# The score products of differential attention: four products of a block in another order

## The chip, the cores and the metric

The kernel runs on one core of a Trainium2 chip. The metric is the time of one execution on the device, in microseconds (us). TensorE is PE in the profile (its weight loads are PEld), VectorE is DVE, ScalarE is ACT, GpSimd is POOL, and SyncE, which issues the transfers, is SP.

## The reference

The kernel computes two layers of a bidirectional trunk over 256 latent tokens, with 256 context tokens in front, at a width of 1024. Each layer has a token mixer of three parts (an mLSTM, an HGRN2 and differential attention) and then a channel mixer: a dense SwiGLU in layer 0, and two of eight SwiGLU experts for each token in layer 1. The change touches the scores of the differential attention only. It has 4 heads; each head has two maps with 64 channels each, and its output is the difference of two softmaxes times the values:

```
s = einsum('ibhqd,ibhkd->ibhqk', q, k) * 64 ** -0.5     # i: the two maps, d: 64 channels
p = softmax(s, axis=-1)
out = einsum('bhqk,bhkv->bhqv', p[0] - lam * p[1], v)
```

In layer 0 the latent tokens attend to all 512 tokens and the context tokens to the 256 context tokens. In layer 1 only the latent's output is needed.

## The kernel before

Everything is worked on in tiles of 128 partitions. All large products are made in float32r, with each fp32 operand split into an upper and a lower part; an exact product is then the sum of three, upper by upper and the two mixed ones. Results go to eight PSUM banks of 128 x 512 (`bank`).

Differential attention goes through tiles of 128 queries (`tt`): four in layer 0 (0 and 1 are context with 256 keys, 2 and 3 are latent with 512), two in layer 1 (both with 512). For each tile it goes through four heads. So there are 16 score blocks in layer 0 and 8 in layer 1.

The operands of a score block lie so that a head needs four products instead of six. The keys of map `i` (`dk`) hold the upper part on one half of the partitions and the lower part on the other half; for map 0 the upper part is on partitions 0 to 63, for map 1 on 64 to 127 (the slices in `both`). The upper part of the queries (`qh`) is on both halves. So one product over all 128 partitions gives upper query by upper key plus upper query by lower key. A second product, over the 64 partitions that hold the upper part of the keys, adds lower query (`ql`) by upper key. Each map has a bank of its own (`pe[0]`, `pe[1]`, called `psc` in the profile).

From there a block goes on like this: VectorE takes the maximum of each row of each map (`mx`, line 1240), ScalarE makes the exponentials and their sums (`E`, `das`), and VectorE combines both maps into one matrix of weights (line 1249 and the two operations after it). `values` transposes these weights on TensorE (line 1259) and copies them (`pT`), and `weighted` multiplies them with the values (`po`) and scales the result (`oo`).

The text of the loop keeps these steps apart: after the scores of a block come two steps of other work that waits for TensorE (`tick(T_DA)`: pieces of the modulation, and the first half of the output projection, `py`), then `onward`, which does `weighted` for an older block and `values` for a block two places back. During the first query tile each block is followed by transposes of the mixer's other outputs (`mix_t`, line 1147). The framework arranges instructions by a planner with costs of its own, except in stretches that are marked as strict; the attention is not one of these. Semaphores and buffers come from the framework too.

Before the attention, the projections (`pr`, `pp`) fill TensorE. After it the rest of the output projection (`py`) follows, then the channel mixer. Weights come through buffers (`raw`) loaded by SyncE's queue, and are split by ScalarE (`whi`) and VectorE (`wlo`). The mLSTM earlier in each layer multiplies keys and queries of two heads over 64 partitions each, one head on each half, each into its own bank (`pS`); it also makes rows of stabilizers by products over 64 partitions (`pM`).

Of the kernel before, what the change touches and what calls it, by code (L numbers as in the profile page):

```python
# [12 lines left out]
F32 = mybir.dt.float32  # L13
# [8 lines left out]
P = 128  # L22
# [10 lines left out]
# column offsets of the fp32 constant table  # L33
# [4 lines left out]
C_TRI = 768                       # [t', t] = 1 where t' < t  # L38
C_IOTA = C_TRI + 128              # row 0..127 on every partition, then 128..255
C_LOW = C_IOTA + 256              # [e, j] = 1 where j < e, 64 columns  # L40
C_SEL = C_LOW + 64                # [32 g + e, e] = 1, 8 columns
C_END = C_SEL + 8
# columns of the sum matrices, per direction: 7 levels, the two outer ones; then ones
# [6 lines left out]
# GpSimd starts no DMAs: its ring of descriptors is as small as it can be  # L50
RING = 1024

# columns of the per-feature table
# [6 lines left out]
# columns of the per-row table  # L60
# [4 lines left out]
# steps of waiting work at each place where a chain leaves gaps  # L65
# [3 lines left out]
def constants():  # L69
# [14 lines left out]
    k = np.zeros((P, 11 * 128), np.float32)           # 7 level masks, the diagonal; two causal masks, the diagonal  # L84
# [16 lines left out]
    m[:, S_OUT:S_OUT + 128] = u > t                       # forward, before the boundary  # L101
    m[:, S_OUT + 128:S_OUT + 256] = u <= t                # forward, after it
    m[:, S_DIR + S_OUT:S_DIR + S_OUT + 128] = u >= t      # backward, queries
    m[:, S_DIR + S_OUT + 128:S_DIR + S_OUT + 256] = u < t  # backward, keys
# [5 lines left out]
def kernel(ctx: ExitStack, tc: tile.TileContext, t: dict, out: bass.AP):  # L110
    nc = tc.nc
    # where a chain of small steps decides, each engine keeps to the order of this text
# [61 lines left out]
    def load_row(gd):  # L174
        """A vector by column, in a place for weights."""
        g = wp.tile([P, 2, D], F32, tag="raw", bufs=4, name="rowg")
        row_in(g, *gd, nc.sync)
        return g
# [9 lines left out]
    def whl(src, put_off=None):  # L188
        """Both parts of weights; the second one by an engine that is named later, if put_off takes it."""
        h, l = hl_tile()  # L190
        ACT(h, src, AF.Copy)
        low = lambda op=TT: op(l, src, h.bitcast(F32), op=ALU.subtract)
        put_off.append(low) if put_off is not None else low()
        return h, l
# [7 lines left out]
    def rstd_of(pool, ss, n, scale, tag, bufs=1):  # L202
        """1 / sqrt(ss * scale + EPS), with a step of Newton's method."""
# [32 lines left out]
    def mod_piece(l, g, n):  # L236
        """A quarter of the rows of 2048 columns of the modulation, four column groups side by side."""
# [26 lines left out]
    def first_mods(c):  # L264
        """Shift and scale of two feature tiles of the first input, four blocks of rows side by side."""
# [23 lines left out]
    work = []  # L289

    def tick(n):
        """Goes on with n steps of the work that waits; the loads of the next piece are sent off early."""
        while n > 0 and work:
            for w in work[:2]:
                if not w[1]:
                    w[1] = True
                    next(w[0])
            try:
                next(work[0][0])
                n -= 1  # L300
            except StopIteration:
                work.pop(0)
# [11 lines left out]
    def mod_affine(l, which):  # L314
        # 0: scale of the mixer's input, 1: gate of its output, 2, 3: the same of the channel mixer
# [9 lines left out]
    def row_out(src, streams):  # L325
        """A vector by feature, for some streams, on its way to gate_in."""
# [8 lines left out]
    def row_in(dst, gd, streams, q=nc.sync):  # L335
        """The vector by column, on every partition."""
# [9 lines left out]
    def scaled(pool, x, bufs=4):  # L346
        """x over its root mean square, for some tiles of tokens."""
# [14 lines left out]
    def pre_steps(pool, xh, l, which, tiles, ks=range(KT)):  # L362
        """Shifts and scales, by feature, of the scaled tiles of tokens."""
# [25 lines left out]
    def post_steps(pool, tiles, cuts=1):  # L389
        """dst = x + gate * norm(ys side by side), for tiles of tokens (ys, x, gate, dst)."""  # L390
# [32 lines left out]
    class Start:  # L423
        """Four feature tiles of the next part: the context's tokens first, as soon as they are there."""
# [9 lines left out]
        def parts(self, sub=TT):  # L434
            """Both parts of the next tile."""
# [14 lines left out]
        def half(self, n, between=None, plan=0, some=range(KT), at=(), lag=0):  # L450
            """The products of half of the tokens; between them, steps of the other half's input."""
# [9 lines left out]
            for j, (w, pp) in enumerate(zip(self.w, self.banks)):  # L461
                late = []
                for k in some:
                    # a bank's first product clears what is written for all of its columns
# [19 lines left out]
    def tail(product, post, pool, X, nxt, fill, plan, start):  # L484
        """The last products of a part, tile by tile of tokens, each with its residual, and the next part's input."""
# [20 lines left out]
    def mixer(l, X, banks=None):  # L506
        """X: the residual stream by token tile (0, 1: context; 2, 3: latent). Its tile holds the mixer's
        output meanwhile."""
# [31 lines left out]
        if l == 0:  # L540
            with tc.tile_pool(name=f"pn{l}", bufs=1) as pn:
# [20 lines left out]
                def turned(xh, first, ks):  # L562
                    """Feature tiles of two tiles of tokens, two of them in a bank; the two that lie together are not used in turn."""
# [19 lines left out]
                def both_pairs(ks):  # L583
                    """The same of all tiles of tokens; a bank for each feature tile."""
# [49 lines left out]
        # -- projections; what the tensor engine does with their results waits until the next one is under way  # L634
# [6 lines left out]
        def fm(ci, n, toks, use, ws=None):  # L641
            """n feature tiles of weights, stationary; use(j, psum) takes [feature, token]."""
# [14 lines left out]
        def tm(ci, tiles, use):  # L657
            """512 columns of weights, moving; use(i, psum) takes [token, column]."""
# [17 lines left out]
        # ============ HGRN2: gates  # L676
# [5 lines left out]
        lbc = hx.tile([P, 2, 4], F32, name="lbc")     # per head pair: ln lb, ln(1-lb), 1-lb, -ln lb  # L682
# [23 lines left out]
        def use_hgf(d):  # L706
            def use(j, pp):
# [5 lines left out]
                STT(s, pp, 0.0, e, op0=ALU.min, op1=ALU.subtract)          # ln sigmoid(f)  # L713
                TT(e, s, pp, op=ALU.subtract)                              # ln sigmoid(-f)
# [6 lines left out]
                STT(s, s, lbc[:, j, 0:1], e, op0=ALU.max, op1=ALU.add)     # ln f  # L721
# [38 lines left out]
        # ============ HGRN2: the recurrence, by halves  # L760
        def sums_of(dst, i, d, c, cols, extra=()):
            """dst [channel, 128]: sums of ln f over tokens of tile i that `cols` picks."""
# [8 lines left out]
        def squares(v, name):  # L771
            """Sums of squares by token and head."""
# [11 lines left out]
        def hgrn():  # L784
            opart = X[:, :, 256:512]
            # boundaries between tiles: context to latent, and between the two tiles of each
# [31 lines left out]
            # the heads of a pair run side by side in the array, each into its own bank  # L818
            half = [slice(0, 64), slice(64, 128)]
            for p0 in range(qt[0], 4, 2):  # L820
# [3 lines left out]
                def weigh(pa, blocks):  # L824
                    """Adds the values of the token tiles that pa's blocks (at, source, query tile) weigh."""
# [32 lines left out]
            # inside a tile: each level's product holds keys at one half of each block, queries at the other;  # L858
            # queries of a pair of heads lie side by side, with zeros where the other head's channels are
# [77 lines left out]
        # ============ mLSTM  # L937
# [29 lines left out]
        # ============ what the rest of the mixer needs from its input  # L967
        dq = hx.tile([P, 4, 512], F32, tag="w8", bufs=3, name="dq")
        # both parts of the keys of each head and map; the lower one at the other half of the partitions
# [18 lines left out]
        def rotated(dst, x, pp):  # L988
            """The rotation of the latent's tokens, of x that pp holds too."""
# [52 lines left out]
        scans(g2, ones_r, g1, ALU.mult, ALU.add)                          # F  # L1042
        TT(g0[R, :], g0[R, :], g2[R, :], op=ALU.subtract)                 # b = i - F
        tick(T_SCAN)
        scans(g1, g0, g0, ALU.max, ALU.max)                               # M
        TT(g2[R, :], g2[R, :], g1[R, :], op=ALU.add)
        tick(T_SCAN)
        ACT(g2[R, :], g2[R, :], AF.Exp, scale=-1.0)                       # exp(-m)
        gh = hg.tile([64, 512], F32R, tag="at", bufs=4, name="gh")
        gl = hg.tile([64, 512], F32R, tag="at", bufs=4, name="gl")  # L1050
        ACT(gh, g1[R, :], AF.Copy, scale=-1.0)                            # -M, in two parts
# [12 lines left out]
        for h in range(4):  # L1064
            if h % 2 == 0:
                # k q of both heads, side by side
# [11 lines left out]
            for d in range(2):  # L1078
# [3 lines left out]
                # -M along rows; the second with the causal mask of each diagonal block  # L1082
# [56 lines left out]
        # ============ differential attention  # L1139
        raw_o = [load(t["w_out"][l, 0, g]) for g in range(2)]  # L1140

        def mix_t(k, i0, i1):
            """Feature tile k of the mixer's output, gated, in two parts, for tokens i0..i1."""
# [61 lines left out]
        def out_first(i):  # L1205
            """Half of the output projection of a tile of tokens."""
# [12 lines left out]
        def queries(tt):  # L1219
            """The upper part of the queries at both halves of the partitions, and the lower part."""  # L1220
# [9 lines left out]
        def scores(tt, h):  # L1230
            sn = 512 if tt >= 2 else 256
            pe = [bank("psc") for _ in range(2)]
            qh, ql = qs[tt]
            for i, a, _ in both:
# [704 lines left out]
```

## Time and profile before

| what | value |
|---|---|
| runs | 2222.86 us median of 3 (2218.38 to 2222.91) |
| profiled execution | span 2226.4 us |
| PE busy | 2138.0 us (96%) |
| PEld busy | 1690.9 us (76%) |
| DVE busy | 1566.9 us (70%) |
| ACT busy | 1249.7 us (56%) |
| transfers | 496.81 MB, mean 223 GB/s |

The profiled execution is one run of its own; its span goes from the first to the last instruction. A busy share is the time in which at least one instruction of the engine was under way. Products on PE are pipelined, so the next one can start before the record of the one before ends; the spacing of two starts says more than the length of one record. PEclk is the granted clock of TensorE, where 1.00 is 2.4 GHz and 0.50 is 1.2 GHz.

### The profile page before, as it was taken

The numbers are of one execution on the slowest core, as the hardware profiler recorded it, in microseconds if no ns is written. First come the engines' busy times: TensorE is split into PE (matmuls) and PEld (weight loads), VectorE is DVE, ScalarE is ACT, GpSimd is POOL, SyncE is SP. The second block draws the span as 40 slices with busy tenths as digits, with TensorE's granted clock in tenths as the row PEclk, the third lists the DMA queues.
The fourth block names the chain that finished last, engine by engine and source line by source line (L and its number), as shares of the span: only waits on it lengthen the run. The fifth ranks groups of instructions, "written<-read, shape, count | busy, mean of one in ns | idle before, by whom it ended". The sixth has DMA issues, their size and how long they took to land.

```text
span 2226.4 us, 27694 instructions
## 1 busy us (share of the span) xinstructions
PE 2138.0 (96%) x10532; PEld 1690.9 (76%) x10532; DVE 1566.9 (70%) x2145; ACT 1249.7 (56%) x1832; POOL 86.8 (4%) x82
## 2 busy tenths in 40 slices
PE   7998998999999999999987999999999999999997
PEld 4877666787788788877866888877777777777775
DVE  4758657672222345766678999788888888888887
ACT  3632435562222335634556787767777677676765
POOL 1000003000000001000112000000000000000000
PEclk9999998799999999999988999999999999999999
DMA  8430444046321331435427999899998999989992
GB/s 302 152 103 30 133 152 151 1 189 237 122 76 38 132 114 42 164 114 189 61 97 311 366 375 346 305 349 350 355 354 322 349 351 350 357 321 355 355 348 105
DMA packets 81356, 496.81 MB, mean 223 GB/s; under 512 B 17728, under 2 KB 18752, under 8 KB 23104
## 3 DMA queue, kind: packets, MB, share of 16 engines
q1 hardware_dynamic: 81216, 494.97, 61.1%
q8 instruction: 84, 1.38, 0.2%
q14 instruction: 56, 0.46, 0.1%
HBM read 492.81 MB, written 2.13 MB: 222 GB/s over the span
## 4 chain that ended last, share of the span: by engine, by line
PE 37%; DVE 7%; ACT 2%; DMA 2%; issue 2%; DVEq 0%; ACTq 0%
PE pg L117 22%; PE py L117 13%; DVE wlo L117 5%; ACT whi L117 1%; DMA raw<-w_eu 1%; PE ph L1710 1%; DMA raw<-w_ed 1%; PE pcb L117 0%; PE px L117 0%; DVE X L117 0%; PE psc L117 0%; PE po L117 0%; DVE qh L1227 0%; DMA X<-w_eu 0%; PE pt L1259 0%
## 5 line engine op out<-in xcount | busy, mean ns | idle before, releaser
L117 DVE TENSOR_TENSOR wlo<-raw,whi 128x1024 fp32r<-128x1024 f32 x815 | 958.9, 1222 | 189.7 <-ACT whi L117 179.6
L117 ACT ACTIVATE whi<-raw 128x1024 fp32r<-128x1024 f32 (+1 forms) x820 | 815.4, 1055 | 272.7 <-PE pgu L117 148.9
L117 PE MATMUL pg<-wlo,TH 128*128 128x512 f32 x896 | 363.4, 406 | 5.7 <-DVE wlo L117 2.0
L117 PE MATMUL pg<-whi,TH 128*128 128x512 f32 x896 | 355.6, 397 | 0.8 <-DVE cf L117 0.8
L117 PE MATMUL pg<-whi,TL 128*128 128x512 f32 x896 | 351.9, 393 | 0.0
L117 PE MATMUL py<-whi,hhl 128*128 128x512 f32 x896 | 289.2, 394 | 0.0
L117 PEld LDWEIGHTS pg<-wlo,TH 128*128 128x128 f32 x896 | 168.3, 188 | 63.5 <-DVE wlo L117 30.2
L117 PEld LDWEIGHTS pg<-whi,TH 128*128 128x128 f32 x896 | 168.3, 188 | 40.4 <-DVE cf L117 1.2
L117 PEld LDWEIGHTS py<-whi,hhl 128*128 128x128 f32 x896 | 168.2, 188 | 38.6
L117 PEld LDWEIGHTS pg<-whi,TL 128*128 128x128 f32 x896 | 168.5, 188 | 35.1
L117 PE MATMUL py<-wlo,hhl 128*128 128x512 f32 x448 | 176.5, 394 | 1.0 <-DVE wlo L117 0.8
L117 ACT ACTIVATE hhl<-ph 128x512 fp32r<-128x512 f32 x56 | 33.3, 595 | 168.7 <-PE ph L1710 168.7
L117 PE MATMUL pgu<-TH,whi 128*128 128x512 f32 x320 | 127.2, 397 | 0.0
L117 PE MATMUL pgu<-TL,whi 128*128 128x512 f32 x320 | 126.6, 396 | 0.0
L117 PE MATMUL pgu<-TH,wlo 128*128 128x512 f32 x320 | 126.5, 395 | 0.0
L117 PE MATMUL pp<-TH,whi 128*128 128x512 f32 (+1 forms) x304 | 116.7, 384 | 0.0
L117 PE MATMUL pp<-TL,whi 128*128 128x512 f32 (+1 forms) x304 | 111.0, 365 | 0.0
L117 PE MATMUL pp<-TH,wlo 128*128 128x512 f32 (+1 forms) x304 | 110.7, 364 | 0.0
L117 PEld LDWEIGHTS py<-wlo,hhl 128*128 128x128 f32 x448 | 84.0, 188 | 21.8 <-DVE wlo L117 2.8
L117 PE MATMUL pm<-raw,sc 128*32 128x512 f32 x384 | 60.5, 650 | 15.6 <-DVE ry L117 9.3
L117 PEld LDWEIGHTS pgu<-TH,whi 128*128 128x128 f32 x320 | 60.1, 188 | 19.2 <-ACT whi L117 3.4
L117 DVE TENSOR_TENSOR hhl<-ph,hhl 128x512 fp32r<-128x512 f32 x56 | 38.6, 689 | 50.9 <-ACT hhl L117 50.8
(342 smaller groups left out, 3229.0 us busy)
## 6 DMA issues: line engine op xcount, KB each, us to landing
raw<-w_eg SPq DMA_DIRECT2D x112, 1024.0 KB, 6.7
raw<-w_eu SPq DMA_DIRECT2D x111, 1024.0 KB, 6.9
raw<-w_ed SPq DMA_DIRECT2D x111, 1024.0 KB, 6.9
raw<-w_mod SPq DMA_DIRECT2D x40, 1024.0 KB, 5.0
raw<-w_fm SPq DMA_DIRECT2D x22, 1024.0 KB, 5.0
raw<-w_fg SPq DMA_DIRECT2D x11, 1024.0 KB, 4.8
raw<-w_fu SPq DMA_DIRECT2D x11, 1024.0 KB, 6.3
raw<-w_fd SPq DMA_DIRECT2D x11, 1024.0 KB, 4.8
```

The source lines that it names most:

```text
L117: ins = op(*args, **kw)
L1710: nc.tensor.transpose(ph[:, j, :], sg[:, j * P:(j + 1) * P], ident)
```

## The change

The four products of a score block are issued in another order. Before, each map had its product over 128 partitions and then its product over 64. Now both products over 128 partitions come first, and then both over 64, the first on partitions 0 to 63 and the second on 64 to 127. Operands, banks, sizes and the accumulation flags of each product are the same. Apart from this the diff only drops comments.

```
     pe = [bank("psc") for _ in range(2)]
     qh, ql = qs[tt]
+    k = [dk[h // 2][:, h % 2, i, 0:sn] for i in range(2)]
+    for i in range(2):
+        MM(pe[i][:, 0:sn], qh[:, i, h, :], k[i], start=True, stop=False)
     for i, a, _ in both:
-        k = dk[h // 2][:, h % 2, i, 0:sn]
-        MM(pe[i][:, 0:sn], qh[:, i, h, :], k, start=True, stop=False)
-        MM(pe[i][:, 0:sn], ql[a, h, :], k[a], start=False, stop=True)
+        MM(pe[i][:, 0:sn], ql[a, h, :], k[i][a], start=False, stop=True)
     mx = hx.tile([P, 2], F32, tag="da_m", bufs=3, name="mx")
```

## Rows read from the trace of the kernel before

**Rows 1.** Page, part 2: busy tenths and granted clock in 40 equal slices

```profile
PE   7998998999999999999987999999999999999997
...
PEclk9999998799999999999988999999999999999999
```

**Rows 2.** Stretch, length, busy us of PE, PEld, DVE, ACT, POOL, clock, DMA, GB/s

```profile
376.94:415.40 38.46, 38.16 (x114) 24.89 (x111) 27.09 (x69) 19.57 (x62) 8.30 (x7) 0.50 0.27 107
384.00:392.00 8.00, 8.00 (x27) 4.68 (x20) 7.69 (x17) 3.45 (x10) 3.79 (x3) 0.50 0.40 140
415.40:440.00 24.60, 24.60 (x132) 18.26 (x131) 17.98 (x49) 15.54 (x43) 0.00 (x0) 1.00 0.01 2
1127.90:1135.60 7.70, 7.70 (x24) 5.30 (x24) 3.71 (x12) 3.43 (x10) 0.73 (x1) 0.50 0.03 13
1135.60:1146.00 10.40, 10.40 (x53) 6.83 (x53) 8.05 (x20) 8.16 (x23) 0.73 (x1) 1.00 0.00 1
```

**Rows 3.** PE's waits, 360 to 460 us, then from 1110 us: us, times, longest

```profile
PE pm L117 <- DMA raw<-w_mod: 5.8, 1, 5.8
PE pt L1259 <- DVE dar L1249: 0.3, 1, 0.3
...
PE pt L1259 <- DVE E L117: 3.1, 1, 3.1
...
PE po L117 <- ACT pT L117: 1.4, 2, 0.7
```

**Rows 4.** Tile psc: its products over 128 partitions; who waited for the tile

```profile
L117 PE MATMUL psc<-dk,qh x48: 279/502/794, 363.8 to 1144.9; 128*128 128x512 f32 x32, 128*128 128x256 f32 x16
...
  DVE mx L1240: 20.2, 23
```

**Rows 5.** Timeline of PE, two blocks of layer 0: start, us, what

```profile
393.54 0.58 PE L117 MATMUL psc<-dk,ql 64*128 64x256 f32 x1
394.05 0.58 PE L117 MATMUL psc<-dk,qh 128*128 128x256 f32 x1
...
405.11 0.79 PE L117 MATMUL psc<-dk,ql 64*128 64x512 f32 x1
405.83 0.79 PE L117 MATMUL psc<-dk,qh 128*128 128x512 f32 x1
```

**Rows 6.** Timeline of PE, a block of layer 1

```profile
1138.38 0.50 PE L117 MATMUL psc<-dk,ql 64*128 64x512 f32 x1
1138.81 0.50 PE L117 MATMUL psc<-dk,qh 128*128 128x512 f32 x1
```

**Rows 7.** Timeline of PE and its weight loads in the mLSTM of layer 0

```profile
293.22 0.40 PE L117 MATMUL pp<-TH,wlo 128*128 128x512 f32 x1
293.54 0.18 PEld L117 LDWEIGHTS pM<-gh,ident_r 64*128 64x128 f32 x1 [0.37 <-ACT whi L117]
293.55 0.50 PE L117 MATMUL pM<-gh,ident_r 64*128 64x512 f32 x1
293.65 0.18 PEld L117 LDWEIGHTS pM<-gl,ident_r 64*128 64x128 f32 x1
293.88 0.39 PE L117 MATMUL pM<-gl,ident_r 64*128 64x512 f32 x1
...
294.11 0.39 PE L117 MATMUL pM<-gh,ident_r 64*128 64x512 f32 x1
```

**Rows 8.** Timeline of PE, products of the output projection at 0.50

```profile
412.79 0.63 PE L117 MATMUL py<-wlo,TH 128*128 128x512 f32 x1
413.21 0.63 PE L117 MATMUL py<-whi,TL 128*128 128x512 f32 x1
```

**Rows 9.** Timeline of weight loads, pairs of mLSTM products over 64 partitions (512 columns, fp32)

```profile
228.73 0.26 PEld L117 LDWEIGHTS pS<-X 64*128 64x128 f32 x2 [0.17 <-DVE bT L1059]
...
229.16 0.26 PEld L117 LDWEIGHTS pS<-X 64*128 64x128 f32 x2 [0.17 <-issue]
```

**Rows 10.** Chain of work that ended last: start, us, what (four fp32 products, 128 columns)

```profile
1140.82 0.44 PE pt L1259 x4
```

## The prediction

> **What bounds the kernel now.** I began with the page's slices of busy time [rows 1]. PE is at nine tenths in most slices, and the granted clock falls below 9 in only four of the 40 (55.7 us each). Three of these hold the changed line: slices 7 and 8 (334 to 445 us, layer 0) and slice 21 (1113 to 1169 us, layer 1). Next come the stretches [rows 2]. From 376.9 to 415.4 us PE is busy for 38.16 of 38.46 us at a granted clock of 0.50 (1.2 GHz); from 415.4 to 440 us all of 24.60 us at 1.00 (2.4 GHz). VectorE has 27.09 us of work in the first of these and does not set the pace. Then the waits [rows 3]: around layer 0's attention PE waits once 5.8 us for a weight transfer, before 376.9 us, and after that 0.3 us in all. Layer 1 is another matter: PE waits 3.1 us for VectorE right before its fourth score block, and later twice for ScalarE (1.4 us together). From the other side [rows 4], VectorE's row maxima waited 23 times and 20.2 us for the score products. So from 376.9 us in layer 0, and from 1127.9 us in layer 1, the order of products on PE sets the pace. Behind it PE stays busy slice after slice, and transfers use 0.01 of their engines from 415.4 to 440 us, so time won there should reach the end of the program.
>
> **What the change touches.** A score block is four products: high part of map 0 over 128 partitions (H0), low part of map 0 over 64 (L0), then H1 and L1. There are 24 blocks: there are 48 H products, 16 of them with 256 columns and 32 with 512 [rows 4], so 8 blocks with 256 columns and 16 with 512. The order becomes H0, H1, L0, L1. Nothing is added: no instruction, DMA or queue entry, and no new wait of PE, since each product goes to the bank that it went to before.
>
> **Price of a change between 128 and 64 rows.** At full clock L0 to H1 is 0.43 us (1138.38 to 1138.81) [rows 6]. Products of one shape follow each other in 0.23 us (293.88 to 294.11) [rows 7]. Each change therefore costs 0.20 us. Rows 7 show where it lies: the last product before a change takes 0.33 (293.22 to 293.55), 0.10 over, and the first one after it 0.33 (293.55 to 293.88), because its weights begin to load only at 293.54. At half clock the spacing is 0.51 us with 256 columns (393.54 to 394.05) and 0.72 with 512 (405.11 to 405.83) [rows 5], against 0.42 for one shape with 512 columns (412.79 to 413.21) [rows 8] and half of that, 0.21, with 256. A change costs 0.30 us there at either width.
>
> A block now has four changes (H0-L0, L0-H1, H1-L1, L1 to the next 128-row product). The new one has two, H1-L0 and L1 to the next. So two go: 0.40 us at full clock, 0.60 at half.
>
> H1 must not expose its weight load after H0, or half a change comes back. Rows 7 show the second weight load at 293.65 running while the first product, on the same 64 rows, is still under way. The Trainium skill ("TensorE: Matmul & The Clock Gate", Part 3: Packing small matmuls) says that a weight load overlaps a running matmul only where the row group differs; by that rule H1 would show its load, about 0.10 us a block, and the sum below would be some 2.5 us smaller (half a change, 0.10 in 8 blocks and 0.15 in 11). The trace disagrees with that rule, and I leave the term out.
>
> **The two low products side by side.** L0 uses partitions 0 to 63 and L1 64 to 127, each in its own bank. The program already has such pairs: for k q of two mLSTM heads, two weight loads come every 0.43 us (228.73, 229.16) with 512 columns in plain fp32 [rows 9], while plain fp32 products of 128 columns take 0.11 us each (four in 0.44) [rows 10], so 0.44 for 512 columns. Two per 0.43 means that the pair runs together. The bounds for the low pair are nothing saved (one after the other) and a whole product (0.23 at full clock; 0.42 and 0.21 at half). I take a start of the second one a weight load later, 0.11 us (293.54 to 293.65) [rows 7], twice that at half clock: saved are 0.12 (512, full), 0.20 (512, half) and nothing (256, half). The Trainium skill (the same page, the same section) has products in distinct row groups start about 4 ns apart; an estimate by it would save the whole product, the upper bound, about 3 us more over all blocks.
>
> **Sum.** The blocks are counted in PE's timeline by clock and width; rows 5 and 6 show one of each kind. Layer 0: its first two blocks, before 376.9 us, win nothing, since PE then waits for the transfer. Six blocks of 256 columns at half clock: 6 x 0.60 = 3.6. Three of 512 at half: 3 x 0.80 = 2.4. Five of 512 at full: 5 x 0.52 = 2.6. Together 8.6 us (7.4 to 11.1 by the bounds). Layer 1: the first three blocks win nothing (VectorE is late after them); of the other five, two begin at half clock (0.80 and about 0.70) and three run at full (1.56): 3.1 us (2.5 to 3.9). All: 11.7 us (9.9 to 15.0).
>
> **What is late next.** VectorE is busy 7.69 of 8.00 us between 384 and 392 [rows 2], so two of the half-clock blocks cannot shrink: minus 1.2 us. In the whole stretch, 38.46 less 6.0 leaves 32.5 us over 27.1 us of VectorE work, so it holds there on average. In layer 1 VectorE has 8.05 and ScalarE 8.16 of 10.40 us, and PE's two waits for ScalarE stand right behind the blocks: I give back 1.1 of 3.1. The first map's maximum starts a little later, since L0 is now third (it ends 0.23 + 0.33 + 0.33 = 0.89 us after the start of a full-clock block, against two spacings, 0.86), and the second map's earlier by about 0.5. Left over: 9.4 us.
>
> **The clock.** It stays at 0.50 from 376.9 to 415.4 us although PE counts as busy throughout, and comes back while PE runs out-projection products (two of them are rows 8), which have no changes. In layer 1 it came back at 1135.6, after 7.7 us [rows 2]. A stream with fewer changes can only look denser. What an earlier return is worth has VectorE as its limit: 32.5 - 27.1 = 5.4 us in layer 0, up to 2 in layer 1; at the other end it is nothing, or a loss if the return slips (last rival). I take 1.6 us, nearer to no change.
>
> Total 11.0 us. The profiled span, 2226.4, is 3.5 us over the median of the timed runs, 2222.86 (2218.38 to 2222.91), so there is nothing around it to add. I take the difference from the median: 2222.9 - 11.0 = 2211.9 us.
>
> **Rivals.**
> *The time turns into waits (0.17).* PE's wins are handed back because VectorE and ScalarE are next in line. For it: the 0.3 us wait for VectorE [rows 3], the full VectorE at 384 to 392, and the two ScalarE waits in layer 1. Against it: VectorE's 20.2 us of waiting for PE. Then only the full-clock blocks of layer 0 and a little of the rest stay, 2.6 + 1 = 3.6 us: 2219.3.
> *The clock returns early (0.15).* Fewer changes lift it inside the blocks: 9.4 + 5.4 + 2 = 16.8 us, so 2206.
> *The order is not kept (0.04).* Outside of its strict parts a planner arranges the program, and it might issue the four products otherwise, or move other work. PE's order in the trace is that of the text, which speaks against it. Nothing changes: 2222.9.
> *Slower: the clock returns later (0.05).* Of the 24.6 us of full-clock PE work up to 440 us [rows 2], each one that runs at 0.50 instead costs about one more. With 14.5 of them caught (most of the five blocks and what stands between them) the loss is 14.5 against the gain of 9.4: 2228. It decides as soon as over 9.4 us are caught. Against it: the run of out-projection products that goes before the return keeps its place in PE's order.
> The forecast itself has 0.59.
>
> **From this the numbers.** A change under 0.2% (4.4 us) cannot be told from none. Faster: 0.59 of the forecast and 0.15 of the early clock, and a fifth of the waits rival (0.03): 0.77. Slower: most of the late clock, and a little for a planner that moves other work: 0.06. The rest, 0.17, is no change. The range runs from 2203 (the upper bounds of the pair with the early clock) to 2220 (the waits rival).
>
> **What would show it.** Right: in a full-clock block H0 to H1 is 0.23 to 0.33 us, the two L start within about 0.1 us of each other, and the block from H0 to the next product takes 1.1 to 1.2 us rather than the four spacings of 0.42 to 0.43; at half clock with 256 columns about 1.4 rather than 2.0. Layer 0's last score product comes some 7 us earlier against its start at 376.9, and the experts' first products some 10 us earlier. The pair is wrong if L0 to L1 is 0.23 or more at full clock. The forecast is wrong if new PE waits for VectorE or ScalarE appear between the blocks, or if the granted clock stands at 0.50 for longer in layer 0, or if the win in attention is lost in a later wait for a transfer.

## The result, and the profile after

The kernel with the new order took 2214.55 us (median of 7 runs, 2211.65 to 2220.39), the kernel before 2223.7 us (7 runs, 2218.38 to 2231.2). The ratio is 0.995, with a 95% interval from 0.9936 to 0.9964: 9.15 us less by the medians, where 11.0 were forecast. The profiled executions lie 12.4 us apart, spans of 2226.4 and 2214.0 us. The one before was among the longer ones of its kernel, so the steps below, which are read from the two traces, add up to 12.4 and not to 9.15. One of the 12 executions of "before, wait filled" further down ran at a mean clock of 0.56 for 3481 us and is left out of that kernel's numbers.

Timeline of PE in the kernel after: start, us, what. First a full-clock block with 512 columns, then a half-clock block with 256, then one with 512; the line behind each is the product that follows the block.

```profile
408.60 0.71 PE L117 MATMUL psc<-dk,qh 128*128 128x512 f32 x2
409.24 0.51 PE L117 MATMUL psc<-dk,ql 64*128 64x512 f32 x2
409.68 0.71 PE L117 MATMUL po<-dv,pT 128*128 128x128 f32 x4
...
390.76 0.78 PE L117 MATMUL psc<-dk,qh 128*128 128x256 f32 x2
391.47 0.58 PE L117 MATMUL psc<-dk,ql 64*128 64x256 f32 x2
391.98 0.58 PE L117 MATMUL po<-dv,pT 128*128 128x128 f32 x1
...
400.88 1.20 PE L117 MATMUL psc<-dk,qh 128*128 128x512 f32 x2
402.01 0.79 PE L117 MATMUL psc<-dk,ql 64*128 64x512 f32 x2
402.74 0.53 PE L117 MATMUL po<-dv,pT 128*128 128x128 f32 x2
```

From the first H to the product behind the block it is now 1.08 us at full clock, 1.22 with 256 columns at half clock, and 1.86 with 512 columns at half clock. The same distances in the kernel before are 1.69, 2.02 and 2.88 us, which are four of the spacings of [rows 5, 6]. The two low products are one entry of two that takes 0.44 us at full clock until the next product starts, as long as one product between two changes (0.43 by [rows 6]). They run together: in the trace's records the second starts 3 to 4 ns behind the first in all 24 blocks, not 0.11 us.

PE's waits in the same stretches as [rows 3], 360 to 460 us, then 1105 to 1134 us (us in total, times, longest):

```profile
PE pm L117 <- DMA raw<-w_mod: 6.8, 1, 6.8
PE po L117 <- ACT pT L117: 2.2, 2, 1.2
PE pt L1261 <- DVE E L117: 1.4, 2, 0.9
PE pt L1261 <- DVE dar L1251: 0.7, 1, 0.7
...
PE pt L1261 <- DVE E L117: 3.5, 2, 3.1
PE po L117 <- ACT pT L117: 0.3, 1, 0.3
```

Layer 0 had 0.3 us of such waits behind the transfer and has 4.3 now (2.2 + 1.4 + 0.7). On the other side the row maxima wait less for the scores; this is the row of tile psc that answers to the last one of [rows 4]:

```profile
  DVE mx L1242: 6.6, 7
```

Stretches of layer 0 from the third score block to the end of the sixteenth, and of layer 1 from the fourth to the end of the eighth, with the columns of [rows 2]. First the kernel before:

```profile
376.94:434.43 57.49, 57.19 (x209) 38.14 (x205) 40.40 (x102) 31.62 (x94) 8.30 (x7) 0.67 0.18 72
1128.63:1145.74 17.11, 17.11 (x72) 11.14 (x71) 10.77 (x30) 11.26 (x29) 1.46 (x2) 0.80 0.01 2
```

Then the kernel after, with four pieces of layer 0 that show the clock:

```profile
377.74:422.62 44.88, 40.61 (x209) 29.50 (x205) 39.35 (x102) 30.23 (x90) 8.16 (x7) 0.80 0.23 91
1119.69:1132.82 13.13, 12.71 (x72) 8.93 (x70) 10.16 (x29) 10.61 (x28) 1.45 (x2) 0.87 0.01 2
...
372.00:384.00 12.00, 8.12 (x38) 4.58 (x38) 8.94 (x18) 5.62 (x17) 5.02 (x4) 0.57 0.98 402
384.00:388.00 4.00, 1.84 (x12) 1.18 (x10) 3.94 (x11) 2.71 (x9) 1.47 (x2) 1.00 0.91 334
388.00:404.00 16.00, 13.89 (x54) 9.89 (x54) 14.54 (x42) 9.75 (x33) 3.92 (x4) 0.57 0.01 4
404.00:440.00 36.00, 36.00 (x213) 29.02 (x213) 24.69 (x69) 24.49 (x66) 0.00 (x0) 1.00 0.00 1
```

The same 209 PE instructions take 44.88 us instead of 57.49, so layer 0 gives 12.61. Their order differs beyond the change in one product of the output projection only, which the planner put behind an earlier block. It splits in four. The lengths of its 14 blocks, read as above, add up to 29.23 us before and 16.76 after, 12.47 less. Of these, 10.9 are the blocks' own: six of 256 columns and three of 512 at half clock and five at full, as before (6 x 0.80 + 3 x 1.02 + 5 x 0.61). The other 1.6 are three blocks that now run at full clock (2 x (1.22 - 0.82) + 1.86 - 1.08). PE's remaining work in the stretch fell from 27.96 (57.19 - 29.23) to 23.85 us (40.61 - 16.76), 4.1 us less with nothing changed in it but the clock: it was at 0.50 up to 415.4 us in [rows 2], and is at 1.00 from 384 to 388 and from 404 us here. Waits took 4.0 us back. So 10.9 + 1.6 + 4.1 - 4.0 = 12.6.

How much of this hangs on the one execution of the kernel before can be seen in a kernel from the experiments below, with the new order in layer 1 alone. Up to layer 1's scores its PE instructions are those of the kernel before, in the same order. Its stretch from the third to the sixteenth block:

```profile
376.93:430.83 53.90, 52.66 (x209) 34.93 (x205) 40.33 (x102) 31.19 (x94) 8.27 (x7) 0.74 0.19 76
```

The old order took 57.49 and 53.90 us here, at a granted clock of 0.67 and 0.74. The new order took 44.88, 44.2 (the second profile) and 44.8 (new order in layer 0 alone). So layer 0 gives 9 to 13 us, by the execution that is taken for before.

From there to the end, in the first two traces: layer 0's third block started 0.8 us later, so the next stage starts 11.8 us earlier (479.46 to 467.64). Layer 1's first block starts only 8.9 us earlier (1115.05 to 1106.11). Layer 1's blocks bring it to 12.5 us at the experts' first products (1194.3 to 1181.8), and 12.4 us reach the end. The 2.9 us lost between the layers lie in layer 1's other mixers, whose code the change does not touch. Stretches there, in the kernel before and then the same work in the kernel after:

```profile
1021.00:1029.00 8.00, 5.46 (x39) 4.23 (x37) 6.36 (x13) 3.75 (x7) 0.00 (x0) 1.00 0.47 160
1029.00:1037.00 8.00, 8.00 (x58) 5.70 (x57) 5.00 (x14) 2.63 (x9) 0.00 (x0) 1.00 0.72 266
```

```profile
985.00:993.00 8.00, 6.95 (x54) 6.32 (x55) 5.67 (x12) 0.00 (x0) 0.00 (x0) 0.79 0.15 65
1009.00:1017.00 8.00, 5.56 (x45) 5.08 (x43) 5.82 (x12) 3.56 (x7) 0.00 (x0) 1.00 0.53 183
1017.00:1025.00 8.00, 8.00 (x29) 3.05 (x29) 3.85 (x8) 1.01 (x4) 0.00 (x0) 0.57 0.44 156
```

In both, PE idles about 2.5 us of the stretch before. In the kernel before the granted clock stays at 1.00 behind that, and 58 PE instructions fit into 8 us; in the kernel after it falls to 0.57, and 29 fit.

### The profile page after: what moved, and what is told of

It is laid out like the page before. It is cut to its first block, busy times and chain, and to the rows that moved or that the text cites. A ratio compares the mean times of both kernels' runs of the same rounds, so it can differ in the third digit from the quotient of the medians.

```text
span 2214.0 us, 27692 instructions
## 1 busy us (share of the span) xinstructions
PE 2118.2 (96%) x10532; PEld 1680.6 (76%) x10532; DVE 1566.6 (71%) x2145; ACT 1249.5 (56%) x1832; POOL 87.7 (4%) x82
## 4 chain that ended last, share of the span: by engine, by line
PE 32%; DVE 10%; DMA 4%; issue 2%; ACT 2%; DVEq 0%; ACTq 0%
PE pg L117 19%; PE py L117 10%; DVE wlo L117 8%; DMA raw<-w_eu 3%; ACT whi L117 1%; DMA raw<-w_ed 1%; PE ph L1712 1%; PE pcb L117 0%; PE px L117 0%; DVE X L117 0%; DVE qh L1227 0%; DVE mx L1242 0%; DMA X<-w_eu 0%; PE po L117 0%; PE psc L117 0%
```

## The experiments

All were timed beside the kernel before, four kernels on each of two chips; the ratio is to the kernel before on the same chip (median 2225.84 and 2226.08 us, 23 executions each) and can differ a little from the quotient of the medians. "Clock" is the mean granted clock from 360 to 430 us of each kernel's profiled execution (one execution each), and "period" the distance from a full-clock block in layer 0 to the next, which takes in all four products and the same work between them. "At half clock" goes over all executions of a kernel and over their whole length: 2 x (1 - mean granted clock) x span, as a mean. Single executions differ widely in it (66 to 103 us in the kernel before on the first chip).

| kernel | median us | ratio, 95% | L0 clock | period us | block, half, 256 | at half clock, us |
|---|---|---|---|---|---|---|
| before | 2225.84, 2226.08 | | 0.68 | 3.05 | 2.02 | 88.4, 89.5 |
| after, run again | 2215.72 | 0.9958 (0.9943 to 0.9972) | 0.88 | 2.41 | 1.21 | 76.4 |
| both L on the same rows | 2220.45 | 0.9980 (0.9966 to 0.9993) | 0.76 | 2.66 | 1.43 | 82.5 |
| H0, L0, L1, H1 | 2211.98 | 0.9945 (0.9927 to 0.9964) | 0.90 | 2.41 | 1.38 | 69.3 |
| all over 128 rows | 2208.52 | 0.9925 (0.9904 to 0.9945) | 0.93 | 2.36 | 1.00 | 62.5 |
| layer 0 alone | 2215.11 | 0.9958 (0.9943 to 0.9974) | 0.83 | | | 75.3 |
| layer 1 alone | 2222.24 | 0.9991 (0.9976 to 1.0006) | 0.76 | | | 87.0 |
| before, wait filled | 2225.59 | 0.9998 (0.9987 to 1.0010) | 0.80 | | | 80.1 |
| after, wait filled | 2212.93 | 0.9944 (0.9928 to 0.9959) | 0.90 | | | 64.9 |

**The kernel after, unchanged.** No edit.

> The changed kernel once more, for a second profile of it. Theory (fewer changes of row shape, low pair side by side): the score blocks take the same time as in the first profile at the same clock (1.08 us with 512 columns at 1.00, 1.86 at 0.50, 1.22 with 256 columns at 0.50), and the time is 0.995 of before, 0.9935 to 0.9965. Rival (much of the difference between the two profiles is where the clock happens to fall): the stretches at 0.50 between the end of layer 0 and layer 1's scores lie elsewhere than in the first profile, and the way from layer 0's last product to layer 1's first score block differs by 2 us or more from the first profile.

Measured: 0.9958, 2215.72 us; the profiled execution is 10.5 us shorter than the one before. Layer 0's scores ended 12.5 us earlier (434.43 to 421.92), and of that 7.6 us were left at layer 1's last pS product (1047.00 to 1039.44): the loss between the layers came again. In 2-us windows the clock was low at 936 to 940, 986 to 992 and 1018 to 1026 us, the last two where the kernel after had it low. So this loss was no accident of one execution; but the kernel with the new order in layer 0 alone, below, has the same PE instructions up to layer 1's scores and shows only a part of it.

**Both low products on the same rows.** The order stays, but L1 reads the partitions of L0, 0 to 63, and so other channels.

```
             for i, a, _ in both:
+                a = both[0][1]
                 MM(pe[i][:, 0:sn], ql[a, h, :], k[i][a], start=False, stop=True)
```

> Both low products use partitions 0 to 63, so that they cannot run side by side; the low part of map 1 is then of the wrong channels. The number of changes of row shape is that of the changed kernel. Theory: the low pair takes one product more, so a block with 512 columns is 1.31 us at 1.00 and 2.29 at 0.50, and 256 columns take 1.43 at 0.50; of 5.2 us more on TensorE (layer 0 3.7, layer 1 1.5) 2 to 5 reach the end: 0.996 to 0.9985 of before. Rival (the second low product hides behind waits for VectorE and ScalarE): the blocks grow by the same, but the time stays within 1 us of the changed kernel, 0.995.

Measured: 0.998, 2220.45 us. Timeline of PE in this kernel, a full-clock block with 512 columns, then a half-clock block with 256:

```profile
415.61 0.72 PE L117 MATMUL psc<-dk,qh 128*128 128x512 f32 x2
416.25 0.73 PE L117 MATMUL psc<-dk,ql 64*128 64x512 f32 x2
416.92 0.50 PE L117 MATMUL py<-whi,TH 128*128 128x512 f32 x1
...
379.69 0.78 PE L117 MATMUL psc<-dk,qh 128*128 128x256 f32 x2
380.40 0.79 PE L117 MATMUL psc<-dk,ql 64*128 64x256 f32 x2
381.12 0.47 PE L1147 MATMUL pt<-ident,X 128*128 128x128 f32 x1
```

Here only the two changes of shape are gone. The block is 1.31 us, 0.38 under the 1.69 of before, and 1.43, 0.59 under 2.02: the prices of 0.40 and 0.60 for two changes hold. From here to the kernel after it is 0.23 (1.31 to 1.08) and 0.21 (1.43 to 1.22): a whole product each time. The two kernels lie 4.7 us apart by their medians, nearly half of the change's gain (10.1 us on this chip). By the medians the two changes less and the pair side by side so have about equal parts in it, each with what it does to the clock and the waits.

**The order H0, L0, L1, H1.**

```
+            MM(pe[0][:, 0:sn], qh[:, 0, h, :], k[0], start=True, stop=False)
             for i, a, _ in both:
-                MM(pe[i][:, 0:sn], ql[a, h, :], k[i][a], start=False, stop=True)
+                MM(pe[i][:, 0:sn], ql[a, h, :], k[i][a], start=(i == 1), stop=(i == 0))
+            MM(pe[1][:, 0:sn], qh[:, 1, h, :], k[1], start=False, stop=True)
```

> Order H0, L0, L1, H1: two changes a block and the low pair side by side, as in the changed kernel, but map 0 is complete after the low pair, one product earlier. Theory: the block on TensorE stays 1.08 us (512 columns at 1.00), and VectorE's first maximum starts 0.2 to 0.4 us earlier, so TensorE's waits for VectorE and ScalarE in layer 0's scores (4.3 us in the changed kernel) shrink by 1 to 2 us: 0.9935 to 0.995 of before. Rival (those waits hang on the second map or on other work of VectorE): same as the changed kernel within 0.5 us.

Measured: 0.9945, 2211.98 us. Timeline of PE, a full-clock block:

```profile
405.57 0.47 PE L117 MATMUL psc<-dk,qh 128*128 128x512 f32 x1
405.98 0.49 PE L117 MATMUL psc<-dk,ql 64*128 64x512 f32 x2
406.40 0.50 PE L117 MATMUL psc<-dk,qh 128*128 128x512 f32 x1
406.74 0.49 PE L117 MATMUL po<-dv,pT 128*128 128x128 f32 x3
```

Two changes and the pair side by side again, only at another place: the block itself is 1.17 us here (1.08 was expected), since both changes now lie inside it, but the period is 2.41 us against 2.43 (408.60 to 411.03) in the kernel after. The first map is complete earlier here, since L0 is second. PE had no wait for ScalarE's pT in layer 0, but 4.1 us for VectorE, against 4.3 us in all in the kernel after. So the time came out as forecast and its reason did not: the waits hardly shrank, and less time was at half clock (69.3 us against 76.4). The intervals of the two orders overlap, so which is faster is not settled.

**All four products over 128 rows.** The low queries get zeros on the other 64 partitions, so the same sums come from products of one shape; no change is left, and no pair runs side by side.

```
+        qz = [op.tile([P, 2, 4, P], F32R, name=f"qz{n}") for n in range(2)]
+        for z in qz:
+            for i, _, b in both:
+                nc.gpsimd.memset(z[b, i].bitcast(F32), 0.0)
...
-                PTT(ql[a], x[a], qh[a, i].bitcast(F32), op=ALU.subtract)
+                PTT(ql[a, i], x[a], qh[a, i].bitcast(F32), op=ALU.subtract)
...
-            for i, a, _ in both:
-                MM(pe[i][:, 0:sn], ql[a, h, :], k[i][a], start=False, stop=True)
+                MM(pe[i][:, 0:sn], ql[:, i, h, :], k[i], start=False, stop=True)
```

> The low part of the queries lies in a tile with zeros on the other half of the partitions, so all four products of a block run over 128 partitions, in the order of before; there is no change of row shape at all. Adds four fills of 64 x 512 on GpSimd per layer. Theory (each change costs 0.20 us at 1.00 and 0.30 at 0.50): a block takes 0.92 to 1.0 us with 512 columns at 1.00, 1.7 to 1.8 at 0.50, and 0.85 to 0.95 with 256 at 0.50, so another 3.5 us of TensorE time go in layer 0; since VectorE is next, 0.5 to 2.5 us of these reach the end: 0.993 to 0.9948. Rival (after the change the stage is bound by VectorE and ScalarE): same as the changed kernel, and TensorE's waits grow by what the blocks shrink.

Measured: 0.9925, 2208.52 us, the lowest median of all, 17.3 us under the kernel before, and a little better than the theory's range; its interval just overlaps that of the kernel after. Timeline of PE, a full-clock block with 512 columns, then a half-clock block with 256 (qz is the low query with zeros):

```profile
404.45 0.48 PE L117 MATMUL psc<-dk,qh 128*128 128x512 f32 x1
404.77 0.40 PE L117 MATMUL psc<-dk,qz 128*128 128x512 f32 x1
405.01 0.39 PE L117 MATMUL psc<-dk,qh 128*128 128x512 f32 x1
405.24 0.39 PE L117 MATMUL psc<-dk,qz 128*128 128x512 f32 x1
405.47 0.59 PE L117 MATMUL po<-dv,pT 128*128 128x128 f32 x3
...
386.20 0.56 PE L117 MATMUL psc<-dk,qh 128*128 128x256 f32 x1
386.56 0.41 PE L117 MATMUL psc<-dk,qz 128*128 128x256 f32 x1
386.77 0.41 PE L117 MATMUL psc<-dk,qh 128*128 128x256 f32 x1
386.99 0.41 PE L117 MATMUL psc<-dk,qz 128*128 128x256 f32 x1
387.20 0.68 PE L117 MATMUL po<-dv,pT 128*128 128x128 f32 x2
```

Products of one shape follow each other in 0.23 to 0.24 us at full clock and 0.21 to 0.22 at half with 256 columns. The spare product costs 0.23. The period is 2.36 us, only 0.07 less than in the kernel after, so the two changes that it replaces cost 0.30 here and not 0.40: the first po behind the block takes 0.21 us to the next one in both kernels, against 0.11 for those behind it, so 0.10 us is paid there with or without a change. PE's waits for ScalarE and VectorE in layer 0 grew to 6.3 us (4.3 in the kernel after), as the rival had said. Most of its lead goes with the clock: 0.93 in layer 0, and over all executions 14 us less at half clock than the kernel after. By an estimate, half a microsecond for each, that is 7 of the 7.2 us between the medians. The Trainium skill ("TensorE: Matmul & The Clock Gate", Part 3: Packing small matmuls) lists that a weight load overlaps a running product only where the row group differs, though its paragraph on the mechanism also lets a load into the background weight buffer go ahead. The trace disagrees with the list: four products on the same 128 rows, each with weights of its own, show no load between them.

**The new order in one layer alone.** Two kernels, with the old order in the other layer.

```
+            if l == 0:          # in the second kernel: l == 1
                 (the four products in the new order)
+            else:
+                for i, a, _ in both:
+                    MM(pe[i][:, 0:sn], qh[:, i, h, :], k[i], start=True, stop=False)
+                    MM(pe[i][:, 0:sn], ql[a, h, :], k[i][a], start=False, stop=True)
```

> The new order in layer 0's 16 score blocks only; layer 1's 8 keep the old one. Theory (the gain of layer 0 is TensorE time of the blocks plus an earlier return of the clock, less new waits): layer 0's score stage ends 12 us earlier than in the kernel before, as in both profiles of the changed kernel, and layer 1's blocks stay at a spacing of 3.04 us; 0.9955 to 0.9975 of before. Rival (the early return of the clock in layer 0 is chance): layer 0's stage ends only 7 to 9 us earlier, with the clock at 0.50 for over 35 us there.

Measured: 0.9958, 2215.11 us. Layer 0's scores ended 13.3 us earlier in the profiled execution (434.43 to 421.17), and 10.5 us were left at the end. Between the layers the clock fell near 937 and 988 us here, but not at 1017, where the kernel after had it at 0.57:

```profile
1017.00:1025.00 8.00, 8.00 (x52) 4.98 (x52) 4.99 (x14) 2.13 (x7) 0.00 (x0) 1.00 0.68 258
```

> The new order in layer 1's 8 score blocks only. Theory: from the fourth block on (start given by VectorE) to the last output-projection product it wins 3 to 4 us, as in the two profiles of the changed kernel; the rest is as before: 0.998 to 0.9992 of before. Rival (VectorE and ScalarE take it all back there): within 1 us of before, and TensorE's waits for ScalarE behind the last block grow by as much.

Measured: 0.9991, 2222.24 us; the interval takes in no change. The profiled execution gained about 4 us between layer 1's pS products and its last scores, 4.8 in the kernel after. By the timed runs layer 0 alone gives as much as both layers (0.9958 each), and layer 1 alone gives 2 us by its ratio, which cannot be told from nothing; the 4 us are of one execution. Its trace holds a second thing: the old order in layer 0 had full clock for a while, here from 388 to 394 us by its timeline, and then lost it again. Stretches of this kernel:

```profile
386.00:396.00 10.00, 8.76 (x39) 6.07 (x39) 8.90 (x25) 7.65 (x26) 2.60 (x2) 0.84 0.29 105
396.00:406.00 10.00, 10.00 (x27) 6.23 (x27) 8.45 (x21) 3.97 (x14) 2.53 (x2) 0.50 0.00 0
```

So the old order does not keep the clock down every time; in PE's ten fully busy us from 396 it is back at 0.50.

**The wait for w_mod filled.** To see whether the 5.8 us wait [rows 3] is what brings the clock down, 28 products of 512 columns, whose bank nobody reads, stand behind layer 0's second block, in the kernel before and in the kernel after.

```
+                if not l and 4 * tt + h == 1:
+                    dm = bank("dm")
+                    for n in range(28):
+                        MM(dm, qs[tt][0][:, 0, 0, :], dk[0][:, 0, 0, :], start=(n == 0), stop=(n == 27))
```

> The kernel before with 28 products of 512 columns added on TensorE (about 6.4 us, into a bank that nobody reads) where it waits for the weight transfer ahead of layer 0's third score block, so that it is not idle there. The planner moves two groups of output-projection products between the blocks. Theory (the idle wait is what takes the clock to 0.50, and it lasts for the 44 us behind it): the clock stays at 1.00 through most of layer 0's scores, VectorE with 27 us of work for 38 us becomes the limit, and the stage ends 6 to 11 us earlier: 0.995 to 0.9975 of before. Rival (the score blocks with their gaps take the clock down anyway): the clock falls to 0.50 within the stage, and the time is within 0.2% of before.

Measured: 0.9998, 2225.59 us: the theory failed, and the rival came. Stretches of this kernel:

```profile
366.00:376.00 10.00, 10.00 (x56) 6.64 (x52) 9.94 (x16) 2.29 (x7) 4.58 (x4) 1.00 0.47 172
376.00:386.00 10.00, 7.50 (x45) 4.14 (x44) 7.52 (x18) 5.01 (x18) 3.75 (x3) 1.00 1.01 425
386.00:396.00 10.00, 9.14 (x29) 6.83 (x29) 7.27 (x20) 6.41 (x23) 2.54 (x2) 0.55 0.09 34
396.00:406.00 10.00, 10.00 (x26) 6.12 (x26) 7.86 (x23) 4.02 (x13) 2.54 (x2) 0.50 0.01 2
```

With the wait filled the clock stays at 1.00 until 386 us. PE then runs into a wait of 2.6 us for ScalarE's pT, and the clock falls and stays down until 414 us, through 20 us in which PE is hardly idle. Over all executions this kernel spent less time at half clock than the kernel before (80.1 against 89.5 us) and was no faster, with 28 products more to do.

> The changed kernel with the same 28 products in the same place. Beside the kernel before with these products it shows what the new order is worth with the clock held up in layer 0. Theory (both count: changes and the low pair, and the clock): 14 blocks save 0.4 us (256 columns) and 0.6 us (512) on TensorE, 7.3 us together, of which VectorE and ScalarE leave 2 to 5 in layer 0, and layer 1 adds 3: 5 to 8 us faster than the other filled kernel, 0.992 to 0.9945 of before. Rival (in layer 0 the new order works only by bringing the clock back): layer 0's stage is as long in both filled kernels within 1 us, and only layer 1's 3 us remain between them.

Measured: 0.9944, 2212.93 us, inside the interval of the kernel after. Two of the stretches in this kernel:

```profile
386.00:396.00 10.00, 9.02 (x37) 7.53 (x38) 7.49 (x24) 6.28 (x23) 2.36 (x2) 0.52 0.11 45
396.00:406.00 10.00, 8.10 (x38) 5.50 (x38) 9.42 (x25) 6.23 (x21) 2.80 (x2) 0.84 0.01 2
```

The clock held until 386 us here too, fell after a wait of 2.3 us for pT, and was low from 386 to 397 and from 403 to 407 us, 14 us against 27. The two filled kernels share the wait and the fall and differ in the order, and in a few products of the output projection that the planner placed otherwise behind 408 us; layer 0's scores end 9.9 us apart (1.8 and 11.7 us earlier than before), the medians 12.7. That is more than the theory's 5 to 8 us; the rival (within 1 us in layer 0) is out.

## Why the prediction was right, and where errors cancelled

**The change of shape: right.** 0.20 and 0.30 us each were taken; the block with both L on the same rows shows 0.38 for two at full clock and 0.59 at half.

**The pair side by side: mis-sized.** The prediction took a start of the second product one weight load later, and so 0.12, 0.20 and 0.00 us saved. Measured is the upper bound that it named: 0.23, 0.42 (2.28 to 1.86 with 512 columns at half clock) and 0.21. The 0.11 us from row 293.54 to 293.65 is the distance of two weight loads for the same rows, and was the wrong row for two products on different rows; [rows 9], two products in the time of one, was the right one. Layer 0's own gain was 10.9 us instead of 8.6. The Trainium skill's offset of about 4 ns (the same page and section) agrees with the trace here, which has the two starts 3 to 4 ns apart.

**What is late next: under-sized.** 1.2 us were given back for layer 0; it was 4.0, and half of the waits were for ScalarE (pT 2.2 us), not for the VectorE (2.1 us) that the prediction had named. Faster blocks and a faster clock bring both engines closer to the bound: VectorE is busy 39.35 of 44.88 us now, and was busy 40.40 of 57.49. The first map is complete 1.08 us after the start of a full-clock block, where it was 0.84 (two spacings), so 0.24 later; the prediction had 0.03. But the order H0, L0, L1, H1, which completes it earlier, had nearly the same waits. In layer 1 the opposite: the prediction gave 1.1 of 3.1 us back, and 3.6 of the 3.98 us (17.11 to 13.13) reached the experts.

**The clock: under-sized in layer 0, missed elsewhere.** 1.6 us were taken for all; layer 0 of the two traces shows 5.7 (1.6 in blocks, 4.1 in other work), about the 5.4 at which the rival "the clock returns early" had been priced. That rival and the waits rival both came.

All executions can be set beside these two traces. The kernel before spent 88 to 90 us at half clock and the kernel after 75 to 76, some 13 us less. Nine blocks that are 0.80 or 1.02 us shorter at half clock are 7.9 of these by themselves. The other 5 us, worth half of that, give an estimate of 2.5 us at most for the clock over the whole program, with the loss between the layers already taken off; in the two traces this was 5.7 - 2.9 = 2.8. So what the clock was worth to the end lies not far from the 1.6 that the prediction took, but as the difference of a gain and a loss that it did not have.

That the shorter blocks are what brings the clock back is supported, not proven: the kernels whose low products run one after the other had 80 to 90 us at half clock over all executions, those in which they run together or over full rows 62 to 76, with 80.1 and 64.9 in the filled pair. In layer 0's profiles the same two groups had a mean clock of 0.68 to 0.80 and of 0.83 to 0.93. A part of each difference is only that the blocks are shorter, and the layer-1-only kernel shows that the old order gets the clock back for a while too. Why it does at one moment and not at another stays open.

**A loss that no step had.** 2.9 us went between the layers with a clock that fell at 986 and 1017 us, in two executions of the new order. Before, in the same work with the same waits, it did not fall there (only once, near 948 us). From the end of layer 0's scores to layer 1's first block it took 680.6 us before and 683.5 and 684.5 in the two executions after, but 681.7 in the kernel with the new order in layer 0 alone, 678.5 in the one with H0, L0, L1, H1, and 679.7 with full rows. The old order itself took 678.5 in the layer-1-only kernel. The PE work there is the same in all of these, and it comes about 12 us or more earlier wherever layer 0 has a new order. So the new order did not lose it every time, and nothing run here tells what decides it: it stays open.

**What would show it.** The blocks came at or under the lower end (1.08 for 1.1 to 1.2, 1.22 for 1.4), layer 0's last scores 12.6 us earlier against their start instead of 7, the experts' first products 12.5 instead of 10. The two L started 3 to 4 ns apart, where 0.1 us was the bound. New waits between the blocks, named as a sign against the forecast, did appear, and were outweighed.

**What was luck.** Against the forecast of 11.0 us the two traces show + 2.3 for the pair, + 4.1 for the clock in layer 0, - 2.8 for the waits there, + 1.6 in layer 1, - 2.9 between the layers and - 0.8 for a third block that began later: together 12.5. The timed runs gave 9.15, which fits with a traced execution of the kernel before that was slow in layer 0 (57.49 us, where the same PE work took 53.90 in another kernel). The mechanism (fewer changes, low products together) was right; that the total came so near is in part that errors of up to 4 us had opposite signs.

## What to carry to other kernels

Where products of 64 and of 128 rows alternate, price each change of shape (0.20 us at full clock, where a product of 512 columns takes 0.23, and 0.30 at half), put products of one shape together, and set two of 64 rows with different rows next to each other: they cost one. Then try zeros on the unused rows before more reordering: four products of one shape took no more time here than three products' time and two changes (period 2.36 against 2.41 to 2.43 us), and that kernel had the lowest median, though not clear of the other new orders. And when a stage gets shorter, look at the clock and at the waits of the stages behind it, since in the profiled execution the code that was not touched gave back a quarter of what layer 0 had won. And take more than one execution of the kernel before: the same instructions took 57.5 and 53.9 us in its layer 0.

## What the runs showed that was not expected

A spare product over full rows (0.23 us) is cheaper than the two changes that it avoids (0.30 in this place). The first product of a block takes 0.32 us to the next one, and 0.36 with 256 columns at half clock, also where all are of one shape: 0.09 and 0.15 more than the others. Little of this is lost time: its record starts 0.03 us (0.07 at half clock) behind the last transpose, while the transposes follow each other in 0.11 (0.21). And a wait of PE of about 2.5 us was followed by a fall of the granted clock in some executions (0.57 from 1017 us in the kernel after, 0.55 from 386 us in the filled kernel before) and by none in others, after the same work.
